# The output norm of a gated delta rule, per token block and head on ScalarE

## The chip, the cores and the metric

The kernel runs on one core of one Trainium2 chip. The metric is the device time of one execution in microseconds; for a kernel that runs several times it is the median of its runs. The core has five engines that work side by side, each through its own list of instructions in order: PE (TensorE, matmuls), DVE (VectorE), ACT (ScalarE), POOL (GpSimd) and SP (SyncE, which here issues the DMA transfers). An instruction starts when the one before it on its engine has started or ended and the semaphores that it waits for are set.

## The reference, cut to what matters

A decoder block of 512 tokens and 2048 channels: a projection of the normalised input, two parallel branches (sliding-window attention and a gated delta rule), a gated sum, an output projection and a last norm. The change is in the delta rule, which has 16 key heads, 32 value heads and chunks of 64 tokens. After the scan over the chunks every value head's output is normalised over its 128 channels:

```python
def rms_norm(x, w):
    xf = x.astype(jnp.float32)
    y = xf * lax.rsqrt(jnp.mean(xf * xf, axis=-1, keepdims=True) + EPS)
    return (y * w.astype(jnp.float32)).astype(x.dtype)

# scan over the chunks, state0 = 0
v_new = u_i - w_i @ state
o = (q_i * exp(g_i)) @ state + qk_i @ v_new
state = state * exp(g_last) + k_dec.T @ v_new

o_d = rms_norm(o_d, dn_norm_w[l]) * jax.nn.silu(z_d)
```

Since the first state is zero, the state after the first chunk is the product alone.

## The kernel before

All matmuls are done in float32 split in two parts: a weight tile of 128 x 1024 is loaded, cast on ACT to `whi` (L162), and the rest `wlo` is subtracted on POOL (L165; `lo_eng` is POOL in this stage). `mm_half` then runs 24 matmuls of 128 x 512 for it: eight with `whi` and the high part of the input (L174), eight with `whi` and its low part (L176), alternating, then eight with `wlo` (L179). Each of `w`, `whi` and `wlo` has three buffers.

PE's order is written out by the program. Side work runs as generators in `flow`: each matmul of a projection counts as one tick, and a generator that yields n goes on n ticks later. So the scan's small matmuls stand at fixed places between those of the projections. The other engines' lists are ordered by a scheduler that looks for what is ready, under `tc.high_priority()` sooner.

The stage of the change loops over 16 key heads `kh`, each with two value heads. While the projections for head kh+1 run, `scan(kh, ...)` goes through the eight chunks of head kh, both value heads side by side. A chunk c lies in token block T = c // 2 and does:

- L555 (PE): `pa` from the state `s_cur`; not in the first chunk.
- L562 (DVE): `rr`, and L566 (ACT): `xq`, both from `pa`. In the first chunk L570 (ACT) copies `rr`.
- L574 (PE): `pb`; L578 and L582 (DVE): `sv`; L585 (DVE), or L587 (ACT) in the first chunk: the output `o`.
- L591, L592 (PE): `pc`; L598 (DVE), or L601 (DVE) in the first chunk: the new state, tile `sn`.

After the last chunk `finish` does the norm over `o`, a tile of 128 tokens by 4 token blocks, 2 heads and 128 channels: square (L609, ACT, into `osq`), sum (L612, DVE, into `so`), a factor with the scale of q (L614, DVE), a reciprocal square root `ro` in ten small DVE steps of 128 x 8 (L193, and three times L195 to L197, in `rsqrt`), and the product of `o` and `ro` in place (L616, DVE). 36 ticks later PE transposes `o` (L621) and L627 multiplies it by the weight and the gate `zs`. The scan of the next head starts while this runs, so that its first chunks share DVE and ACT with `finish`. ACT also runs L295 and L643 (the value path), L649 (`zs`), L522, L524, L530 and L531 (`prepare`) and L288 (a gate tile after heads 3, 7 and 11); POOL copies `kc` (L511).

Of the kernel before, what the change touches and what calls it, by code (L numbers as in the profile page):

```python
# [8 lines left out]
F32 = mybir.dt.float32  # L9
F32R = mybir.dt.float32r  # L10
I32 = mybir.dt.int32
AF = mybir.ActivationFunctionType
ALU = mybir.AluOpType
AX = mybir.AxisListType

P = 128
S = 512
NT = S // P
# [61 lines left out]
def hybrid_block(  # L80
# [21 lines left out]
    pe, dve, act, pool = nc.tensor, nc.vector, nc.scalar, nc.gpsimd  # L102
# [10 lines left out]
    def new_pool(stack, name, bufs, side="left"):  # L113
        return stack.enter_context(tc.tile_pool(name=name, bufs=bufs, side=side, reuse_waits="tile"))
# [4 lines left out]
    def bank(tag, bufs=1):  # L119
        return ps.tile([P, S], F32, name=tag, bufs=bufs)  # L120
# [70 lines left out]
    def rsqrt(pl, y, v, n):  # L191
        t = pl.tile([P, n], F32, name="nrt")
        dve.tensor_scalar(y.bitcast(I32), v.bitcast(I32), -0.5, 1597463007.0, ALU.mult, ALU.add)  # L193
        for _ in range(3):
            dve.scalar_tensor_tensor(t, y, -0.5, v, ALU.mult, ALU.mult)  # L195
            dve.tensor_tensor(t, t, y, ALU.mult)
            dve.scalar_tensor_tensor(y, t, 1.5, y, ALU.add, ALU.mult)  # L197
# [288 lines left out]
    with ExitStack() as st:  # L486
        pv = new_pool(st, "pv", 2)
# [57 lines left out]
        def scan(kh, vb, zs):  # L545
            slab, tq, kth, ktl = got.pop(kh)
            o = pv.tile([P, NT, 2, P], F32, name="o")
            s_cur = None
            v2 = slice(2 * kh, 2 * kh + 2)
            for c in range(8):  # L550
                T, p = divmod(c, 2)
                rk, rq = (H0, H1) if p == 0 else (H1, H0)
                if c:
                    xp = bank("pa").rearrange("p (h e) -> p h e", h=4)[:, 0:2, :]
                    pe.matmul(xp, slab[:, T, 2 * p:2 * p + 2, :].rearrange("d b i -> d (b i)"), s_cur,  # L555
                              start=True, stop=True)
                    rr = rrs[p]
                    xq = pv.tile([P, 2, P], F32, name="xq")
                    with tc.high_priority():
                        for h in range(2):  # L560
                            vh = 2 * kh + h
                            dve.scalar_tensor_tensor(rr[rk, h, :], xp[rk, h, :], nbeG[rk, T, vh:vh + 1],  # L562
                                                     vb[rk, T, h, :], ALU.mult, ALU.add)
                    for h in range(2):
                        vh = 2 * kh + h
                        act.activation(xq[rq, h, :], xp[rq, h, :], AF.Copy, scale=eGs[rq, T, vh:vh + 1])  # L566
                    yield 8
                else:
                    rr = rrs[p]
                    act.copy(rr[rk], vb[rk, T])  # L570
                    yield 4
                yp = bank("pb").rearrange("p (h e) -> p h e", h=4)[:, 0:2, :]
                for h in range(2):
                    pe.matmul(yp[:, h, :], tq[:, h * 4 + T, :], rr[:, h, :], start=True, stop=True)  # L574
                if c < 7:
                    sv = pv.tile([P, 2, P], F32R, name="sv")
                    with tc.high_priority():
                        dve.tensor_tensor(sv[rk], yp[rk], eSuf[rk, T, v2].unsqueeze(2).broadcast_to([64, 2, P]),  # L578
                                          ALU.mult)
                        for h in range(2):  # L580
                            vh = 2 * kh + h
                            dve.scalar_tensor_tensor(sv[rq, h, :], yp[rk, h, :], eSuf[rk, T, vh:vh + 1],  # L582
                                                     sv[rk, h, :].bitcast(F32), ALU.mult, ALU.subtract)
                if c:
                    dve.tensor_tensor(o[rq, T], xq[rq], yp[rq], ALU.add)  # L585
                else:
                    act.copy(o[rq, T], yp[rq])  # L587
                yield 10
                if c < 7:
                    su = bank("pc").rearrange("p (h e) -> p h e", h=4)[:, 0:2, :]  # L590
                    pe.matmul(su, kth[:, T, p, :], sv, start=True, stop=False)  # L591
                    pe.matmul(su, ktl[:, T, p, :], sv, start=False, stop=True)  # L592
                    s_new = pv.tile([P, 2, P], F32, name="sn")
                    with tc.high_priority():
                        if c:
                            for h in range(2):
                                vh = 2 * kh + h
                                dve.scalar_tensor_tensor(s_new[:, h, :], s_cur[:, h, :], eTot[p][:, T, vh:vh + 1],  # L598
                                                         su[:, h, :], ALU.mult, ALU.add)
                        else:  # L600
                            dve.tensor_copy(s_new, su)  # L601
                    s_cur = s_new
                    yield 8
            flow.start(finish(kh, o, zs))

        def finish(kh, o, zs):
            osq = pv.tile([P, NT * 2, P], F32, name="osq", bufs=1)
            ov = o.rearrange("p t h e -> p (t h) e")
            act.activation(osq, ov, AF.Square)  # L609
            so = pv.tile([P, 8], F32, name="so")  # L610
            ro = pv.tile([P, 8], F32, name="ro")
            dve.tensor_reduce(so, osq, AX.X, ALU.add)  # L612
            so4 = so.rearrange("p (t h) -> p t h", h=2)
            dve.scalar_tensor_tensor(so4, so4, 1.0 / P, cq[:, :, kh:kh + 1].broadcast_to([P, NT, 2]), ALU.mult, ALU.add)  # L614
            rsqrt(pv, ro, so, 8)
            dve.tensor_tensor(ov, ov, ro.unsqueeze(2).broadcast_to([P, 8, P]), ALU.mult)  # L616
            yield 36
            for h in range(2):
                tp = bank("tr", 2)
                for T in range(NT):  # L620
                    pe.transpose(tp[:, T * P:(T + 1) * P], o[:, T, h, :], ident)  # L621
                od = pv.tile([P, S], F32, name="od")
                tv = tp.rearrange("p (t c i) -> p t c i", t=NT, c=2)
                dv = od.rearrange("p (t c i) -> p t c i", t=NT, c=2)
                zv = zs[:, h, :].rearrange("p (t c i) -> p t c i", t=NT, c=2)
                for p in range(2):
                    dve.scalar_tensor_tensor(dv[:, :, p, :], tv[:, :, 1 - p, :], dnw, zv[:, :, p, :], ALU.mult, ALU.mult)  # L627
                nc.sync.dma_start(od_d[KT + 2 * kh + h], od)
                yield 6
# [4 lines left out]
        for kh in range(NK):  # L634
            vb = pv.tile([P, NT, 2, P], F32, name="vb")
            zs = pv.tile([P, 2, S], F32, name="zs", bufs=3)
            flow.start(prepare(kh), 24 if kh else 60)
            for h in range(2):
                vh = 2 * kh + h

                def then(acc):
                    y = conv(acc, 32 + vh, pv)
                    act.activation(y, y, AF.Silu)  # L643
                    after = (lambda kh=kh, vb=vb, zs=zs: scans.add(scan(kh, vb, zs))) if h else None
                    flow.start(to_tokens(y, vb, h, vh, after))

                proj(w_in[T_DN + 32 + vh], then)
            for h in range(2):
                proj(w_in[T_DZ + 2 * kh + h], lambda acc: act.activation(zs[:, h, :], acc, AF.Silu))  # L649
                if h == 0 and kh + 1 < NK:  # L650
                    load_head(kh + 1)
            if kh in GATE_KH:
                gate_tile(pv, 47 - n_gate)
                n_gate += 1
# [339 lines left out]
```

## Time and profile before

| | us |
|---|---|
| median of 3 runs | 2913.93 (2913.84 to 2914.82) |
| profiled execution, its own time | 2914.18 |
| its span, first to last instruction | 2912.4 |
| PE busy | 2850.0 (98%) |
| DVE busy | 1762.9 (61%) |
| ACT busy | 1028.6 (35%) |
| POOL busy | 555.8 (19%) |
| delta-rule scan stage | 850 to 1830 of the span |

Matmuls overlap on PE: the busy time of one is longer than the distance to the next, and an idle PE is one that had no matmul in work. A row in order of time has the start in us, the duration in us, the engine, the line, the operation, output and input with their shapes, and xN where N rows were merged; in brackets stands how long the engine was idle before it and what ended that. A row of a group has, after the count, the total of its busy time in us and the mean of one in ns, then the idle time before it.

### The profile page before, as it was taken

The page shows a single profiled execution, that of the slowest core. Times are in us where ns is not written, and L with a number is a line of the kernel's source. Part 1 is how long each engine was busy: PE and PEld are TensorE (multiplying, and loading weights), DVE is VectorE, ACT ScalarE, POOL GpSimd, SP SyncE. Part 2 cuts the span into 40 slices and gives each one's busy share as a digit, 9 for nine tenths or more (in the row PEclk, how much of TensorE's full clock was granted, in tenths as well). Part 3 has the DMA queues.
Part 4 walks back from the last instruction along what each step waited for, and adds up shares of the span by engine and source line. Part 5 has one row for each costly group of instructions (what it writes and reads, how often), then busy time and mean ns, then how long its engine had stood idle before and what let it go on. Part 6 is the DMA issues. An engine that isn't in the chain of part 4 may idle for free.

```text
span 2912.4 us, 36773 instructions
## 1 busy us (share of the span) xinstructions
PE 2850.0 (98%) x13594; PEld 2370.9 (81%) x13594; DVE 1762.9 (61%) x3520; ACT 1028.6 (35%) x1645; POOL 555.8 (19%) x464
## 2 busy tenths in 40 slices
PE   7999999999999999999999999999999999999998
PEld 7778888888888888888878888877788888888887
DVE  6686667979825555555555554478884455455434
ACT  5532222232333343334333333355553222122222
POOL 2310000000033334333334333024230000000010
PEclk9999999999999999999999999999999999999999
DMA  3344444353553333333333322424237555554533
GB/s 132 115 123 142 135 136 151 125 207 116 174 153 100 103 110 103 105 98 116 98 109 109 104 89 94 133 87 113 91 109 225 172 174 163 156 163 147 181 100 103
DMA packets 184628, 376.07 MB, mean 129 GB/s; under 512 B 65505, under 2 KB 82273, under 8 KB 183041
## 3 DMA queue, kind: packets, MB, share of 16 engines
q1 hardware_dynamic: 184448, 373.72, 40.7%
q8 instruction: 108, 1.77, 0.3%
q14 instruction: 72, 0.58, 0.1%
HBM read 316.97 MB, written 54.59 MB: 128 GB/s over the span
## 4 chain that ended last, share of the span: by engine, by line
PE 88%; DVE 8%; ACT 2%; issue 1%; POOL 0%; DMA 0%; SPq 0%; ACTq 0%; DVEq 0%
PE acc L179 24%; PE acc L176 24%; PE acc L174 24%; PE pa L555 2%; PE pb L574 2%; PE fo L902 1%; PE fo L900 1%; PE fo L901 1%; PE acc L247 1%; PE tr L529 1%; DVE ptl L764 1%; DVE o L616 1%; DVE ro L197 1%; DVE wlo L165 1%; DVE ad L381 1%
## 5 line engine op out<-in xcount | busy, mean ns | idle before, releaser
L174 PE MATMUL acc<-hT_hi,whi 128*128 128x512 f32 x2592 | 1038.5, 401 | 0.0
L176 PE MATMUL acc<-hT_lo,whi 128*128 128x512 f32 x2592 | 1018.7, 393 | 0.0
L162 ACT CAST whi<-w 128x1024 fp32r<-128x1024 f32 x446 | 467.7, 1049 | 1166.5 <-PE acc L176 940.4
L179 PE MATMUL acc<-hT_hi,wlo 128*128 128x512 f32 x2592 | 685.1, 398 | 2.2 <-DVE wlo L165 2.2
L165 POOL TENSOR_TENSOR wlo<-w,whi 128x512 fp32r<-128x512 f32 x284 | 363.3, 1300 | 1231.8 <-PE acc L179 643.7
L165 DVE TENSOR_TENSOR wlo<-w,whi 128x512 fp32r<-128x512 f32 x608 | 424.0, 720 | 261.1 <-ACT whi L162 204.5
L176 PEld LDWEIGHTS acc<-hT_lo,whi 128*128 128x128 f32 x2592 | 488.6, 188 | 92.8
L174 PEld LDWEIGHTS acc<-hT_hi,whi 128*128 128x128 f32 x2592 | 488.3, 188 | 92.9
L179 PEld LDWEIGHTS acc<-hT_hi,wlo 128*128 128x128 f32 x2592 | 479.6, 188 | 98.1 <-DVE wlo L165 3.1
L176 PE MATMUL acc<-dl,whi 128*128 128x512 f32 x768 | 298.8, 389 | 0.0
L174 PE MATMUL acc<-dh,whi 128*128 128x512 f32 x768 | 298.8, 389 | 0.0
L179 PE MATMUL acc<-dh,wlo 128*128 128x512 f32 x768 | 189.7, 389 | 0.0
L297 DVE SCALAR_TENSOR_TENSOR cy<-acc,cw,cy 128x511 f32<-128x511 f32 (+2 forms) x192 | 142.8, 744 | 62.9 <-ACT cy L295 60.0
L863 DVE TENSOR_TENSOR gd<-acc,gl 128x512 f32<-128x512 f32 x80 | 55.3, 691 | 188.7 <-PE acc L179 188.7
L176 PEld LDWEIGHTS acc<-dl,whi 128*128 128x128 f32 x768 | 144.2, 188 | 30.0
L179 PEld LDWEIGHTS acc<-dh,wlo 128*128 128x128 f32 x768 | 144.1, 188 | 29.9
L174 PEld LDWEIGHTS acc<-dh,whi 128*128 128x128 f32 x768 | 144.1, 188 | 29.9
L562 DVE SCALAR_TENSOR_TENSOR rr<-pa,nbeG,vb 64x128 f32<-64x128 f32 x224 | 69.0, 348 | 143.2 <-PE pa L555 143.0
L920 POOL TENSOR_TENSOR y<-y,fw 128x512 f32<-128x512 f32 x12 | 18.9, 1605 | 658.7 <-ACT sqy L918 658.7
L566 ACT ACTIVATE xq<-pa,eGs 64x128 f32<-64x128 f32 x224 | 68.9, 356 | 170.1 <-DVE rr L562 167.6
L578 DVE TENSOR_TENSOR sv<-pb,eSuf 64x256 fp32r<-64x256 f32 x112 | 46.9, 418 | 116.7 <-PE pb L574 116.4
L467 DVE TENSOR_TENSOR m<-m,tm 128x62 f32<-128x62 f32 (+30 forms) x124 | 106.4, 858 | 2.8
(264 smaller groups left out, 3182.2 us busy)
## 6 DMA issues: line engine op xcount, KB each, us to landing
w<-w_in SPq DMA_DIRECT2D x326, 512.0 KB, 3.5
w<-w_dn SPq DMA_DIRECT2D x64, 512.0 KB, 3.5
gl<-ga_d SPq DMA_DIRECT2D x96, 256.0 KB, 2.6
w<-w_att SPq DMA_DIRECT2D x32, 512.0 KB, 3.8
w<-w_out SPq DMA_DIRECT2D x32, 512.0 KB, 3.5
of<-od_d SPq DMA_DIRECT2D x48, 256.0 KB, 3.9
kq_d<-slab SPq DMA_DIRECT2D x16, 512.0 KB, 2.8
ga_d<-gt SPq DMA_DIRECT2D x32, 256.0 KB, 3.8
```

The costliest lines, as they stand in the source:

```text
L162: act.copy(hi, w)
L165: lo_eng[0].tensor_sub(lo[:, r], w[:, r], hi[:, r].bitcast(F32))
L174: pe.matmul(acc, hi[:, k, :], rhi[k], start=first and k == 0, stop=False)
L176: pe.matmul(acc, hi[:, k, :], rlo[k], start=False, stop=False)
L179: pe.matmul(acc, lo[:, k, :], rhi[k], start=False, stop=last and k == n - 1)
L297: dve.scalar_tensor_tensor(y[:, sh:], acc[:, 0:S - sh], cw[:, t, 3 - sh:4 - sh], y[:, sh:], ALU.mult, ALU.add)
L467: dve.tensor_tensor(m[:, 0:jj, jj + 1:], m[:, 0:jj, jj + 1:], tm, ALU.add)
L555: pe.matmul(xp, slab[:, T, 2 * p:2 * p + 2, :].rearrange("d b i -> d (b i)"), s_cur, start=True, stop=True)
L562: dve.scalar_tensor_tensor(rr[rk, h, :], xp[rk, h, :], nbeG[rk, T, vh:vh + 1], vb[rk, T, h, :], ALU.mult, ALU.add)
L566: act.activation(xq[rq, h, :], xp[rq, h, :], AF.Copy, scale=eGs[rq, T, vh:vh + 1])
L574: pe.matmul(yp[:, h, :], tq[:, h * 4 + T, :], rr[:, h, :], start=True, stop=True)
L863: dve.tensor_tensor(gd, acc, gl, ALU.mult)
```

## The change

Three edits, all in the scan stage:

- The square of `finish` becomes eight instructions on ACT, one for each token block and head (128 x 128), each of which also gives the sum over its channels as a column of `so`; the sum on DVE goes.
- The product of `o` and `ro` becomes eight instructions on ACT, each with its column of `ro` as scale; the product on DVE goes.
- The copy of the first state of each head goes from DVE to ACT.

```diff
                         else:
-                            dve.tensor_copy(s_new, su)
+                            act.copy(s_new, su)
 ...
         def finish(kh, o, zs):
-            osq = pv.tile([P, NT * 2, P], F32, name="osq", bufs=1)
             ov = o.rearrange("p t h e -> p (t h) e")
-            act.activation(osq, ov, AF.Square)
             so = pv.tile([P, 8], F32, name="so")
             ro = pv.tile([P, 8], F32, name="ro")
-            dve.tensor_reduce(so, osq, AX.X, ALU.add)
+            for n in range(8):
+                osq = pv.tile([P, P], F32, name="osq", bufs=2)
+                act.activation(osq, ov[:, n], AF.Square, accum_out=so[:, n:n + 1])
             so4 = so.rearrange("p (t h) -> p t h", h=2)
             dve.scalar_tensor_tensor(so4, so4, 1.0 / P, cq[:, :, kh:kh + 1].broadcast_to([P, NT, 2]), ALU.mult, ALU.add)
             rsqrt(pv, ro, so, 8)
-            dve.tensor_tensor(ov, ov, ro.unsqueeze(2).broadcast_to([P, 8, P]), ALU.mult)
+            for n in range(8):
+                act.activation(ov[:, n], ov[:, n], AF.Copy, scale=ro[:, n:n + 1])
```

The new squares stand at L612 and the new products at L617 of the changed kernel; lines behind `finish` have a number higher by one (L644 for L643, L650 for L649, L628 for L627). PE's order is the same row for row. Those of ACT and DVE change where `finish` of one head meets the start of the next.

ACT, where `finish` of head 0 meets the first chunk of head 1, before:

```order
L566 ACTIVATE xq<-pa,eGs 64x128 x2
L609 ACTIVATE osq<-o 128x1024
L570 COPY rr_6246<-vb 64x256
L162 CAST whi<-w_7137 128x1024
L587 COPY o<-pb 64x256
L649 ACTIVATE zs<-acc 128x512
L566 ACTIVATE xq<-pa,eGs 64x128 x2
```

and now, where `w_7157` is the same weight tile as `w_7137`:

```order
L566 ACTIVATE xq<-pa,eGs 64x128 x2
L612 ACTIVATE osq,so<-o 128x128 x2
L570 COPY rr_6246<-vb 64x256
L617 ACTIVATE o<-o,ro 128x128 x8
L587 COPY o<-pb 64x256
L650 ACTIVATE zs<-acc 128x512
L162 CAST whi<-w_7157 128x1024
L601 COPY sn<-pc 128x256
L566 ACTIVATE xq<-pa,eGs 64x128 x2
```

The last two of the eight squares stay there (the other six went forward into the scan), the eight products come in ahead of L587 and `zs`, the weight cast goes behind them, and the state's copy is last. At the next head's `finish` (head 1) the cast stands ahead of the products, and after head 2 `zs` does so too.

DVE at the same place (head 0 to head 1), before:

```order
L612 TENSOR_REDUCE so<-osq 128x8
L614 SCALAR_TENSOR_TENSOR so<-so,cq 128x8
L193 TENSOR_SCALAR ro<-so 128x8
...
L578 TENSOR_TENSOR sv<-pb,eSuf 64x256
L195 SCALAR_TENSOR_TENSOR nrt<-ro,so 128x8
L582 SCALAR_TENSOR_TENSOR sv<-pb,eSuf,sv 64x128 x2
L196 TENSOR_TENSOR nrt<-nrt,ro 128x8
L197 SCALAR_TENSOR_TENSOR ro<-nrt,ro 128x8
L616 TENSOR_TENSOR o<-o,ro 128x1024
L601 COPY sn<-pc 128x256
L562 SCALAR_TENSOR_TENSOR rr_6247<-pa,nbeG,vb 64x128 x2
```

and now:

```order
L614 SCALAR_TENSOR_TENSOR so<-so,cq 128x8
L193 TENSOR_SCALAR ro<-so 128x8
...
L195 SCALAR_TENSOR_TENSOR nrt<-ro,so 128x8
L196 TENSOR_TENSOR nrt<-nrt,ro 128x8
L197 SCALAR_TENSOR_TENSOR ro<-nrt,ro 128x8
L578 TENSOR_TENSOR sv<-pb,eSuf 64x256
L582 SCALAR_TENSOR_TENSOR sv<-pb,eSuf,sv 64x128 x2
L562 SCALAR_TENSOR_TENSOR rr_6247<-pa,nbeG,vb 64x128 x2
```

Reduce, product and state copy are gone, and `sv` (L578, L582), which stood among the last small steps of `rsqrt`, now stands behind all of them.

## Prediction

> **What bounds the kernel now.** I read the page first, then the busy times by stretch, then TensorE's waits in one stretch, and last the rows in order of time around one such wait. All sums are against the profiled execution: 2914.18 us, 1.8 us around its span, and 0.25 us above the median 2913.93 us. Its span:
>
> ```profile
> span 2912.4 us, 36773 instructions
> ```
>
> The edit lies in the scan of the delta rule, which runs from about 850 to 1830 us. Columns: length of the stretch, then busy us of PE, PEld, DVE, ACT, POOL, and the granted clock:
>
> ```profile
> 850.00:1830.00 980.00, 962.15 (x4817) 801.49 (x4816) 539.65 (x1338) 364.91 (x608) 357.29 (x290) 1.00 0.34 103
> ```
>
> TensorE is idle for 17.85 of 980 us at full clock, so no edit of vector work can win much more than that here. Who makes it wait (us in total, times, longest):
>
> ```profile
> PE pa L555 <- DVE sn L601: 13.2, 12, 1.5
> PE pc L591 <- DVE sv L582: 4.2, 5, 1.2
> ```
>
> So nearly all of it is one wait: the second chunk of a head wants the first state, sn, that L601 copies. I call the point where `finish` of head kh runs while head kh+1 starts a changeover, and sort the 16 by kh modulo 4: A (0, 4, 8, 12), B (1, 5, 9, 13), C (2, 6, 10, 14), D (3, 7, 11), and the last head. The 12 waits sit in A, B and C; D, after a gate tile, has none. The first A, engine by engine:
>
> ```profile
> 912.63 0.41 DVE L585 TENSOR_TENSOR o<-xq,pb 64x256 f32<-64x256 f32 x1 [1.74 <-PE pb L574]
> ...
> 914.17 1.22 DVE L612 TENSOR_REDUCE so<-osq 128x8 f32<-128x1024 f32 x1 [0.48 <-ACT osq L609]
> 915.43 0.17 DVE L614 SCALAR_TENSOR_TENSOR so<-so,cq 128x8 f32<-128x8 f32 x1
> 915.63 0.17 DVE L193 TENSOR_SCALAR ro<-so 128x8 int32<-128x8 int32 x1
> ...
> 918.27 1.17 DVE L197 SCALAR_TENSOR_TENSOR ro<-nrt,ro 128x8 f32<-128x8 f32 x1
> 919.48 2.27 DVE L616 TENSOR_TENSOR o<-o,ro 128x1024 f32<-128x1024 f32 x1
> 921.67 0.41 DVE L601 COPY sn<-pc 128x256 f32<-128x256 f32 x1
> ```
> ```profile
> 913.08 1.06 ACT L609 ACTIVATE osq<-o 128x1024 f32<-128x1024 f32 x1 [1.48 <-DVE o L585]
> ...
> 915.80 1.05 ACT L162 CAST whi<-w 128x1024 fp32r<-128x1024 f32 x1 [1.36 <-issue]
> 918.13 0.37 ACT L587 COPY o<-pb 64x256 f32<-64x256 f32 x1 [1.28 <-DVE sv L582]
> 918.52 0.60 ACT L649 ACTIVATE zs<-acc 128x512 f32<-128x512 f32 x1
> ```
> ```profile
> 913.76 0.60 POOL L511 COPY kc<-slabv 128x512 f32<-128x512 f32 x1
> ...
> 918.13 2.54 POOL L165 TENSOR_TENSOR wlo<-w,whi 128x512 fp32r<-128x512 f32 x2 [3.76 <-issue]
> ```
> ```profile
> 920.58 0.39 PE L176 MATMUL acc<-hT_lo,whi 128*128 128x512 f32 x1
> 922.13 0.70 PE L555 MATMUL pa<-sn,slabv 128*128 128x256 f32 x2 [1.17 <-DVE sn L601]
> 922.48 0.59 PE L174 MATMUL acc<-hT_hi,whi 128*128 128x512 f32 x1
> ```
>
> VectorE runs in order. Reduce, eleven small steps (one each 0.20 us) and the scaling L616 stand ahead of L601, which ends at 922.08, while ScalarE has nothing to do after 919.12. TensorE's own loss is more than the 1.17 us shown. The same step where it does not wait:
>
> ```profile
> 863.69 0.39 PE L176 MATMUL acc<-hT_lo,whi 128*128 128x512 f32 x1
> 863.91 0.59 PE L555 MATMUL pa<-sn,slabv 128*128 128x256 f32 x2
> 864.16 0.59 PE L174 MATMUL acc<-hT_hi,whi 128*128 128x512 f32 x1
> ```
>
> There L555 starts 0.22 us after L176 and L174 0.25 us after that; in A it is 1.55 and 0.35. The loss is 1.33 + 0.10 = 1.43 us: each wait costs about 0.27 us more than its row says. L555 was wanted at 920.58 + 0.22 = 920.80.
>
> Two of VectorE's rows are stretched: L197 took 1.17 and L616 2.27 while POOL's wlo ran (918.13 to 920.67).
>
> ```profile
> L197 DVE SCALAR_TENSOR_TENSOR ro<-nrt,ro x48: 166/166/1220, 916.2 to 1823.8; 128x8 f32<-128x8 f32 x48
> L616 DVE TENSOR_TENSOR o<-o,ro 128x1024 f32<-128x1024 f32 x16 | 23.8, 1486 | 0.5
> ```
>
> A step of 166 ns that takes up to 1220 ns looks held until the POOL operation beside it (1.27 us each) ends. The Trainium skill ("SBUF — State Buffer", Who interferes with whom) says that a VectorE instruction with two SBUF inputs and a GpSimd one that reads SBUF fully block each other, and that ScalarE never waits on anyone. The rows above agree. By that rule the scaling on ScalarE is never held; were it held there as L616 was, by 1.05 us, the four A would give 4.2 us less.
>
> **The change, priced.** Removed from VectorE per head: L612 1.22, L616 1.49 and L601 0.41 us, 50 us in all, of which only what stands before L601 in A, B and C is on TensorE's path. Added on ScalarE; the nearest rows:
>
> ```profile
> L918 ACT ACTIVATE sqy<-y 128x512 f32<-128x512 f32 x15 | 9.4, 628 | 25.2 <-DVE y L916 25.2
> L733 ACT ACTIVATION_READ_ACCUMULATOR sc<-sc,nm 128x1 f32 x128 | 23.9, 187 | 0.0
> L934 ACT ACTIVATE y<-y,rsf 128x512 f32<-128x512 f32 x8 | 5.3, 716 | 9.2 <-DVE rsf L209 9.2
> ```
> ```profile
> 2873.02 1.34 ACT L934 ACTIVATE y<-y,rsf 128x512 f32<-128x512 f32 x2 [2.33 <-DVE rsf L209]
> ```
>
> - Square: 1.06 us at 1024 elements (L609) and 0.628 at 512 give 0.85 ns per element, so 0.30 us at 128, and 0.187 for the read of the sum. Two L934 take 1.34 rather than 1.43, so neighbours overlap by 0.09: 0.31 us per square with its read. Six of a head's eight run while its scan goes on; only two wait for its last block.
> - Scale: 0.716 - 384 x 0.00085 = 0.39 us, 0.30 from one to the next; eight take 2.4 us. Ends: 0.26 (were the overlap larger) and 0.39 (none); I take 0.30, the nearest row's own.
> - State copy: as L587, the same 256 elements per partition out of PSUM, 0.37 us.
>
> ScalarE's busy time rises by 16 x (8 x 0.49 + 8 x 0.39 - 1.06 + 0.37), about 102 us, to 467 of 980. That is covered: the casts L162 run when one of three buffers comes free, two weight tiles ahead of TensorE (24 matmuls, 0.22 us apart as in the rows above, are 5.3 us per tile), so A's cast, which moves from 915.80 to 919.8, is not seen. Without that cover each late cast would cost its lateness. The transposes that read o stand 36 ticks after `finish`; o is ready at 919.0 in A, not at 921.75. POOL's and SP's orders stay, and the order holds 31 table loads before and after.
>
> Now the sn time in each class, in the new order. **A**: o is done at 913.04, two squares and reads until 913.8; if POOL's L511 (until 914.36) holds the first small step, eleven steps end at 916.6. Scales to 919.0; L587, zs and the weight cast, which now stands between zs and sn, start at 919.0, 919.3 and 919.8; sn 920.75 to 921.1, against 920.80 wanted: 0.3 late, a loss of 0.4 instead of 1.43.
>
> **B and C** (first of each):
>
> ```profile
> 972.34 0.41 DVE L585 TENSOR_TENSOR o<-xq,pb 64x256 f32<-64x256 f32 x1 [0.76 <-PE pb L574]
> ...
> 1032.13 0.41 DVE L585 TENSOR_TENSOR o<-xq,pb 64x256 f32<-64x256 f32 x1 [1.46 <-PE pb L574]
> ```
> ```profile
> 974.14 1.05 ACT L162 CAST whi<-w 128x1024 fp32r<-128x1024 f32 x1 [0.29 <-PE acc L176]
> ...
> 1034.81 0.60 ACT L649 ACTIVATE zs<-acc 128x512 f32<-128x512 f32 x1 [0.24 <-PE acc L179]
> ...
> 1105.45 0.60 ACT L649 ACTIVATE zs<-acc 128x512 f32<-128x512 f32 x1 [0.81 <-PE acc L179]
> ```
> ```profile
> 976.47 2.54 POOL L165 TENSOR_TENSOR wlo<-w,whi 128x512 fp32r<-128x512 f32 x2 [3.01 <-issue]
> ```
> ```profile
> 979.83 0.39 PE L176 MATMUL acc<-hT_lo,whi 128*128 128x512 f32 x1
> 981.29 0.70 PE L555 MATMUL pa<-sn,slabv 128*128 128x256 f32 x2 [1.07 <-DVE sn L601]
> ...
> 1041.56 0.70 PE L555 MATMUL pa<-sn,slabv 128*128 128x256 f32 x2 [1.53 <-DVE sn L601]
> ...
> 1107.31 0.59 PE L555 MATMUL pa<-sn,slabv 128*128 128x256 f32 x2
> ...
> 1768.76 0.38 PE L591 MATMUL pc<-sv,kth 128*128 128x256 f32 x1 [1.21 <-DVE sv L582]
> ```
>
> B: squares end 973.5, ro 975.75, before POOL's wlo at 976.47; scales to 978.2, L587, zs, sn done 979.4; wanted 980.05. C: ro 1035.5, after zs; scales to 1037.95, sn done 1038.6; wanted about 1039.9. D: sn follows zs, done 1106.35; wanted 1107.31. So B and C lose their waits and D gets none. Head 14, a C, waits at L591 (1.21) and 0.27 at L555, because small steps were held; the new order puts sv behind all eleven steps and the same POOL operation falls among them, so I give it half back.
>
> **Sum**: A 4 x (1.43 - 0.40) = 4.1; B 4 x (1.07 + 0.27) = 5.4; C three waits that with head 14's 0.27 make 13.2 - 4 x 1.17 - 4 x 1.07, so 4.0, plus 3 x 0.27 = 4.8; head 14 half of 1.21 + 0.27 + 2 x 0.27 = 1.0. Together 15.3 us: 2914.18 - 15.3 = 2898.9, or 2898.6 as a median. The other four L591 waits stay: they come from head preparation.
>
> **Rivals.** A difference under 0.2% (5.8 us) can hardly be told from none here.
>
> 1. *All of it goes*: A isn't late, head 14 is clean (17.9 us saved) and the four other L591 waits vanish with VectorE's lighter load (4 x 1.0). 2892. For it: A misses by only 0.3. Against: those four follow a cast held by POOL. 12%.
> 2. *Between*: scales don't overlap (0.39, 0.7 us later): A loses 1.1, B 0.2, about 11 saved, 2903; up to 2908 if part of the copy also waits for a cast. 12%.
> 3. *The wait changes engines*: sn now stands behind eight scales in order, as it stood behind L616. If ScalarE's chain is 1.5 us later than I have it, A loses 1.9 (4 x 0.5 more than now), B 0.95, C 0.3, and D, short of 0.55, gets a wait of 0.65 thrice: net 2 us, 2912, no change. The Trainium skill ("ScalarE: Activation LUTs", Rules for kernel authors) says to multiply on VectorE and not on ScalarE, which speaks for this rival; by rows, 2.4 us for eight scales against 1.22 for an unheld L616 agrees that ScalarE is slower, and only its idle time saves the change. 12%.
> 4. *Slower, by POOL's hold*: the eleven small steps stay on VectorE and sv now stands behind all of them. From 0.7 us later than I have them, B's and C's last steps meet both wlo operations (976.47 to 979.01 in B): sv ends about 980.1, L591 waits 2.1 us, then L555 0.3. B loses 2.8 instead of 1.34, C about 2.9 instead of 1.6; with A's 4.1 saved that is 5.6 lost, 2919.5. Head 14's row shows that it happens. 8%.
>
> **Chances.** The likeliest, at 56%, is 2898.6, with 2895 to 2903 as its own range. Cases 1 and 2 make it 80% for 2891.5 to 2908, the range; 3 and 4 are left out. Faster by over 0.2%: 56 + 12 + 12 = 80%; within: 14% (case 3 and part of 4); slower 6%.
>
> **What would show it.** L555 has no wait on sn in B and C, and 0 to 0.4 us in A; squares of about 0.30 and scales of about 0.39 us; the eleven steps end before wlo starts in B; TensorE idle 3 to 6 us in the stretch, not 17.85. It would be wrong if L591 waits for sv in B or C, if L555 waits in D, if scales start more than 1 us after ro, or if TensorE starts to wait for a weight cast.

## The result, and the profile after

| | before | changed |
|---|---|---|
| median, us | 2913.89 (2912.09 to 2914.82, 4 runs) | 2899.11 (2897.90 to 2899.86, 4 runs) |
| ratio, 95% interval | | 0.995, 0.9935 to 0.9966 |
| profiled execution, its own time | 2914.18 | 2897.90 |

The change makes the kernel 14.8 us faster (2913.89 - 2899.11), and the interval of the ratio lies below 1. The forecast was 2898.6 us. Of the five runs behind the median of 2896.86 us in the table of the experiments, one took 3154.43 us at a granted clock of 0.849; the other four lie between 2895.78 and 2897.40 us. The page of the changed kernel begins:

```profile
span 2896.1 us, 37062 instructions
```

The scan stage, with the columns as before (length, then busy us of PE, PEld, DVE, ACT, POOL, then the granted clock):

```profile
850.00:1830.00 980.00, 975.26 (x4884) 814.16 (x4883) 484.02 (x1297) 438.77 (x995) 351.74 (x289) 1.00 0.35 106
```

VectorE has 56 us less to do than before, ScalarE 74 more, and TensorE is idle for 4.74 us of the 980 instead of 17.85. TensorE's waits in the stage (us in total, times, longest):

```profile
PE pc L591 <- DVE sv L582: 3.5, 5, 0.7
PE pa L555 <- ACT sn L601: 0.8, 4, 0.2
```

Twelve waits of 13.2 us for sn have become four of 0.8 us. The groups of the new instructions on ScalarE (total of busy time, mean of one in ns, idle time before):

```profile
L617 ACT ACTIVATE o<-o,ro 128x128 f32<-128x128 f32 x128 | 39.2, 389 | 16.1 <-DVE ro L197 15.7
L612 ACT ACTIVATE osq<-o 128x128 f32<-128x128 f32 x128 | 38.8, 304 | 97.5 <-DVE o L585 97.2
L612 ACT ACTIVATION_READ_ACCUMULATOR osq<-o 128x1 f32 x128 | 23.9, 187 | 0.0
L601 ACT COPY sn<-pc 128x256 f32<-128x256 f32 x16 | 5.9, 370 | 0.1
```

The first A in order of time, on VectorE, ScalarE and TensorE:

```profile
910.06 0.41 DVE L585 TENSOR_TENSOR o<-xq,pb 64x256 f32<-64x256 f32 x1 [1.74 <-PE pb L574]
...
911.23 0.58 DVE L614 SCALAR_TENSOR_TENSOR so<-so,cq 128x8 f32<-128x8 f32 x1
...
913.66 0.17 DVE L197 SCALAR_TENSOR_TENSOR ro<-nrt,ro 128x8 f32<-128x8 f32 x1
914.08 0.42 DVE L578 TENSOR_TENSOR sv<-pb,eSuf 64x256 fp32r<-64x256 f32 x1 [0.25 <-PE pb L574]
```
```profile
913.87 2.46 ACT L617 ACTIVATE o<-o,ro 128x128 f32<-128x128 f32 x8 [2.31 <-DVE ro L197]
916.35 0.37 ACT L587 COPY o<-pb 64x256 f32<-64x256 f32 x1
916.74 0.60 ACT L650 ACTIVATE zs<-acc 128x512 f32<-128x512 f32 x1
917.23 1.04 ACT L162 CAST whi<-w 128x1024 fp32r<-128x1024 f32 x1
918.17 0.38 ACT L601 COPY sn<-pc 128x256 f32<-128x256 f32 x1
```
```profile
918.01 0.39 PE L176 MATMUL acc<-hT_lo,whi 128*128 128x512 f32 x1
918.59 0.70 PE L555 MATMUL pa<-sn,slabv 128*128 128x256 f32 x2 [0.20 <-ACT sn L601]
```

VectorE now has nothing but eleven small steps ahead of sv, and sv waits for its own input. ScalarE is the engine on which sn stands last: eight scales, a copy (L587), the gate `zs` and a weight cast, 4.3 us without a gap. sn ends at 918.54 and L555 waits 0.20 us for it.

### The profile page after: what moved, and what is told of

Its sections match the earlier page's. It is cut to its first block, busy times and chain, and to the rows that moved or that the text cites. A ratio compares the mean times of both kernels' runs of the same rounds, so it can differ in the third digit from the quotient of the medians.

```text
span 2896.1 us, 37062 instructions
## 1 busy us (share of the span) xinstructions
PE 2845.1 (98%) x13594; PEld 2368.0 (82%) x13594; DVE 1703.8 (59%) x3472; ACT 1098.7 (38%) x2029; POOL 552.4 (19%) x464
## 4 chain that ended last, share of the span: by engine, by line
PE 91%; DVE 5%; ACT 2%; issue 1%; POOL 0%; DMA 0%; ACTq 0%; DVEq 0%
PE acc L179 25%; PE acc L176 25%; PE acc L174 25%; PE pb L574 2%; PE pa L555 2%; PE fo L902 1%; PE fo L901 1%; PE fo L903 1%; PE acc L247 1%; PE tr L529 1%; DVE ptl L765 1%; PE pc L591 1%; DVE ad L381 1%; DVE wlo L165 1%; PE tr L622 0%
## 5 line engine op out<-in xcount | busy, mean ns | idle before, releaser
L578 DVE TENSOR_TENSOR sv<-pb,eSuf 64x256 fp32r<-64x256 f32 x112 | 47.0, 419 | 119.4 <-PE pb L574 119.2
```

## The experiments

The prediction took VectorE's order as given and asked what stands ahead of sn. It left open which part of the change is needed, and why VectorE was late at all. Theory: sn is late by what stands ahead of it on its engine, so each part alone is enough and the parts do not add up. Rivals: VectorE's load is what counts; or the copy itself has to leave VectorE. The medians and ratios come from runs beside the kernel before; the last three columns are read from each profile. The waits are those that the profile lists, and it lists no idle time below 0.15 us. Listed waits for other tiles come to 1.3 us in the kernel with the scales twice and to 0.6 us at most in the others.

| kernel | median, us | ratio to before, 95% interval | L555, first to last, us | waits of L555, us (times) | waits of L591 |
|---|---|---|---|---|---|
| before | 2913.4 to 2914.5 | | 951.3 | 13.2 (12) | 4.2 (5) |
| the change | 2899.11 | 0.9935 to 0.9966 | 936.7 | 0.8 (4) | 3.5 (5) |
| copy alone | 2898.59 | 0.9937 to 0.9962 | 936.2 | 0 | 4.2 (6) |
| squares and scales, no copy | 2896.86 | 0.9927 to 0.9954 | 934.6 | 0 | 3.5 (5) |
| scales alone | 2899.37 | 0.9937 to 0.9962 | 936.3 | 0 | 4.1 (5) |
| squares alone | 2899.05 | 0.9933 to 0.9960 | 936.5 | 0 | 4.8 (5) |
| the change, scales twice | 2923.86 | 1.0022 to 1.0046 | 961.7 | 19.3 (12) | 3.8 (6) |
| squares, scales and ktl's copies | 2892.54 | 0.9912 to 0.9939 | 930.3 | 0 | 0.7 (1) |
| the change, wlo on VectorE | 2891.27 | 0.9908 to 0.9935 | 929.9 | 0 | 0 |
| before, wlo on VectorE | 2888.75 | 0.9899 to 0.9926 | 927.4 | 0 | 0 |
| copy alone, wlo on VectorE | 2889.53 | 0.9901 to 0.9928 | 927.7 | 0 | 0 |
| squares, scales, ktl, wlo on VectorE | 2890.05 | 0.9904 to 0.9931 | 928.2 | 0 | 0 |

The column of L555 is the distance between the first and the last of its 224 matmuls in the stage, as in these two rows (before, then changed); what happens ahead of the stage is not in it:

```profile
L555 PE MATMUL pa<-sn,slabv x224: 376/377/483, 863.9 to 1815.2; 128*128 128x256 f32 x112
```
```profile
L555 PE MATMUL pa<-sn,slabv x224: 377/377/484, 861.4 to 1798.1; 128*128 128x256 f32 x112
```

**One part at a time.** The copy alone, on the kernel before:

```diff
-                            dve.tensor_copy(s_new, su)
+                            act.copy(s_new, su)
```

> The kernel before with one edit: the first state copy sn of a head (L601) is made on ScalarE; squares, norm and scales stay on VectorE. Theory (only what stands ahead of sn on its own engine counts): sn now stands right behind the two small ScalarE operations of the head and comes before it is wanted in every class of changeover, so all twelve waits of L555 go: 13.2 us and twelve restarts of 0.27 us, 16.4 us in all, about 2897.5 us, a little below the change itself; L591's waits for sv stay as before, head 14's among them. Rival (VectorE's load in the changeover is what counts, and one copy is 0.2 us of it): less than 3 us saved, about 2911 us.

It saved 15.9 us (2914.47 - 2898.59). No wait of L555 is left, and all that TensorE waits for sv stays (total, times, longest):

```profile
PE pc L591 <- DVE sv L582: 4.2, 6, 1.2
```

sn now ends 1.25 to 1.27 us before L555 starts in every A, B and C. So one copy of 0.37 us, moved to an engine where it does not stand behind the norm, gives as much as the whole change. The other way round, the changed kernel with that copy back on VectorE:

```diff
-                            act.copy(s_new, su)
+                            dve.tensor_copy(s_new, su)
```

> The changed kernel with one part undone: squares with their sums and the scales are on ScalarE, but the first state copy sn stays on VectorE. Theory: with the eight scales and the square gone from VectorE, sn stands behind the eleven small steps and sv alone, at about 919.6 us in the first changeover, 1.2 us before it is wanted; the waits of L555 go, head 14's wait halves: about 2897 us. Rival (the copy has to leave VectorE): about 2913 us.

17.6 us saved; the copy does not have to leave. Then the scales alone on ScalarE (squares, sum and copy as before):

```diff
-            dve.tensor_tensor(ov, ov, ro.unsqueeze(2).broadcast_to([P, 8, P]), ALU.mult)
+            for n in range(8):
+                act.activation(ov[:, n], ov[:, n], AF.Copy, scale=ro[:, n:n + 1])
```

> The kernel before with one edit: the eight scales of a finished block are on ScalarE; square, sum and the first state copy stay on VectorE. Theory: sn comes right behind ro, about 2.5 us earlier than before: in time in class A (saves 4 x 1.43 = 5.7 us), 0.05 us late in B (saves about 4.6 us), 0.4 us late in C (saves about 3.3 us); some 13.6 us in all, about 2900.3 us. Rival (the parts of the change add up, and this one is a third of it): about 2909 us.

15.1 us saved, 1.5 more than forecast: B and C were to be late by 0.05 and 0.4 us. B is in time, with 0.09 us between the end of sn and L555. In the first C L555 starts 0.06 us after sn ends, which is the distance that it has in the waits of before too (0.05 to 0.06 us), so there sn is still late, by about 0.1 us, too little to be listed. The first B on VectorE:

```profile
973.99 1.22 DVE L197 SCALAR_TENSOR_TENSOR ro<-nrt,ro 128x8 f32<-128x8 f32 x1
...
975.65 0.17 DVE L197 SCALAR_TENSOR_TENSOR ro<-nrt,ro 128x8 f32<-128x8 f32 x1
975.73 0.42 DVE L601 COPY sn<-pc 128x256 f32<-128x256 f32 x1
```

The small step is still held at 1.22 us, and sn is just in time all the same. Last, the squares with their sums alone on ScalarE, the scales and the copy on VectorE:

> The kernel before with one edit: the eight squares with their sums are on ScalarE; the scales and the first state copy stay on VectorE, the scales now ahead of sv in VectorE's order. Theory: VectorE is done with the scales early and sn still comes in time, so L555's waits go; but sv stands behind the scales, so if anything holds the scales (1.22 us on paper), L591 waits for sv instead: about 2897.5 us if not held, up to 1.5 us for each of eleven changeovers more if held, 2897 to 2914 us. Rival (the parts add up): about 2909 us, with both waits shortened but none gone.

15.4 us saved. L555 waits nowhere. The scaling stands ahead of sv in every A, B and C and takes 1.22 us there. The price named for sv fell on head 14 only, where two small steps ahead of the scaling are held (L591 waits 2.0 us, the longest of its waits in any kernel here):

```profile
1748.77 1.29 DVE L195 SCALAR_TENSOR_TENSOR nrt<-ro,so 128x8 f32<-128x8 f32 x1
1750.10 1.22 DVE L196 TENSOR_TENSOR nrt<-nrt,ro 128x8 f32<-128x8 f32 x1
...
1751.55 1.22 DVE L616 TENSOR_TENSOR o<-o,ro 128x1024 f32<-128x1024 f32 x1
1752.69 0.41 DVE L578 TENSOR_TENSOR sv<-pb,eSuf 64x256 fp32r<-64x256 f32 x1
```

The parts alone give 15.9, 15.1 and 15.4 us, together 14.8. They do not add up; each brings sn to TensorE in time or nearly so, and coming earlier than that wins nothing.

**How near the change is to its limit.** The scales made twice, and the first copy taken out of its priority so that the scheduler keeps it behind all sixteen:

```diff
+            for n in range(8):
+                osq = pv.tile([P, P], F32, name="osq", bufs=2)
+                act.activation(osq, ov[:, n], AF.Copy, scale=ro[:, n:n + 1])
             for n in range(8):
                 act.activation(ov[:, n], ov[:, n], AF.Copy, scale=ro[:, n:n + 1])
```

> The changed kernel with each scale made twice on ScalarE (first into a scratch tile, then in place), and the first state copy without its priority, so that it stays behind all sixteen scales. ScalarE gets 2.45 us more per head, 39 us in all, and stays under half busy. Theory (what stands ahead of sn on its engine, by the margins of the changed kernel's trace): class A had a wait of 0.20 and loses 2.45 less the 0.95 of one weight cast that now stands behind sn, 1.5 each, 6.0 in four; B had a margin of 0.59 and waits 1.86 more and a restart of 0.27, 8.5 in four; C had 1.10 and waits 1.35 and a restart, 4.9 in three; head 14 had none and loses 2.45; class D's rr copy stands behind the scales and may cost 0 to 1.3 each. Together 22 to 26 us: 2921 to 2925 us, slower than the kernel before. Rival (ScalarE is idle more than half the time and has room): 2899 us.

2923.86 us, 10.5 above the kernel before (2913.36 beside it), within the forecast. ScalarE is busy for 464.50 of 980 us:

```profile
850.00:1830.00 980.00, 955.17 (x4769) 794.43 (x4769) 476.18 (x1284) 464.50 (x1100) 351.89 (x289) 1.00 0.32 102
```
```profile
PE pa L555 <- ACT sn L601: 19.3, 12, 2.4
```

The single waits were 1.64 to 1.66 us in A (1.7 forecast), 1.70 in B (1.86), 1.18 to 1.20 in C (1.35) and 2.36 in head 14 (2.45). An engine that is idle more than half the time costs 25 us against the change when one copy stands behind 2.45 us more of other work in each head.

**Why VectorE was late.** The four L591 waits of head preparation were put down to a cast held beside GpSimd. On the kernel with squares and scales moved, ktl's casts go to ScalarE:

```diff
-                dve.tensor_copy(ktl[r2, :, p, :], ktl[r, :, p, :].bitcast(F32))
                 yield 8
+            for p, r, r2 in ((0, H0, H1), (1, H1, H0)):
+                act.copy(ktl[r2, :, p, :], ktl[r, :, p, :].bitcast(F32))
```

> The kernel with squares and scales on ScalarE and the state copy on VectorE (the best so far), and the two copies of ktl to the other half of the partitions (L525) made on ScalarE too, behind the second copy of kth. Theory: the four remaining waits of L591 in the head preparation come from L525, which VectorE takes 1.15 us for beside GpSimd's wlo and 0.42 us otherwise, with sv behind it; with L525 gone they go, 4 x (0.69 + 0.27) = 3.8 us, and on ScalarE it is not held (about 0.6 us each): about 2893 us. Rival (the second subtraction of ktl, which stands between sv's two instructions, is what makes sv late): under 1.5 us saved, 2895.5 us or more.

2892.54 us; the four waits are gone and head 14's is left (the edit moves the lines by one, so L592 here is L591). But the edit did more than the forecast says. In the changed kernel, the first of the four places on VectorE:

```profile
994.90 1.14 DVE L525 CAST ktl<-ktl 64x512 fp32r<-64x512 f32 x1
996.07 0.43 DVE L578 TENSOR_TENSOR sv<-pb,eSuf 64x256 fp32r<-64x256 f32 x1
996.42 0.69 DVE L523 TENSOR_TENSOR ktl<-tr,kth 64x512 fp32r<-64x512 f32 x1
997.14 0.63 DVE L582 SCALAR_TENSOR_TENSOR sv<-pb,eSuf,sv 64x128 fp32r<-64x128 f32 x2
```

The second subtraction of ktl (L523, 0.69 us) stands between the two instructions of sv, as the rival says, and with the cast gone the scheduler puts it behind both, at all four places. The hold (1.14 - 0.42 = 0.72 us) and L523 are each as long as the wait (0.69 us), so this kernel does not tell the theory from the rival, though its time is the one that the theory gave.

What TensorE still waits for sv, and the casts on ScalarE, where each takes the same time, whatever runs beside it (ns: least, median, most):

```profile
PE pc L592 <- DVE sv L583: 0.7, 1, 0.7
```
```profile
L527 ACT CAST ktl<-ktl x32: 612/616/619, 843.1 to 1711.9; 64x512 fp32r<-64x512 f32 x32
```

Then the other side of the same pair: in the changed kernel, GpSimd's wlo goes to VectorE, which has 284 more instructions for it.

```diff
-        lo_eng[0] = pool
+        lo_eng[0] = dve
```

> The changed kernel with the low parts of the weights (L165) on VectorE instead of GpSimd in this stage: 284 instructions of 0.685 us, some 195 us more on VectorE. Theory (a VectorE instruction with two SBUF inputs is held while GpSimd's wlo runs): no small step of the norm and no L525 is longer than 0.2 and 0.43 us any more (up to 1.29 and 1.17 us now). The time is the price of the load on VectorE and is not forecast closer than 2895 to 2960 us. Rival (the long ones are long for another reason): they stay at 1.2 us.

The first run gave 2891.94 us, and the median of five with it is 2891.27:

> The changed kernel with L165 on VectorE in this stage, timed in rounds beside the others: 2892 us as in its one run, since the five waits of L591 are gone and two waits of L555 of 0.2 us are left.

The cast on VectorE, in the kernel before and in this one:

```profile
L525 DVE CAST ktl<-ktl x30: 420/424/1164, 883.8 to 1732.7; 64x512 fp32r<-64x512 f32 x30
```
```profile
L525 DVE CAST ktl<-ktl x30: 420/422/425, 883.1 to 1713.0; 64x512 fp32r<-64x512 f32 x30
```

No instruction of the norm is longer than 0.62 us any more. The forecast of 0.2 us for all of them was too strict: GpSimd still makes `kc` (L511, 0.61 us), and some steps meet it. This shows the hold itself: with wlo off GpSimd, the long casts and steps are gone. It does not single out the cast as the cause of the four waits of L591, since here too L523 no longer stands between the instructions of sv.

The profile of the first run lists two waits of 0.2 us for sn, that of the timed kernel none for sn or sv. But in its four A sn is still late, by too little to be listed (the first of them):

```profile
918.86 0.37 ACT L601 COPY sn<-pc 128x256 f32<-128x256 f32 x1
```
```profile
919.28 0.70 PE L555 MATMUL pa<-sn,slabv 128*128 128x256 f32 x2
```

L555 starts 0.05 us after sn ends, as in the waits. ScalarE's chain ahead of sn is the one of the changed kernel, and the hold has no part in it. The distance of the L555 fell by 6.8 us (936.7 - 929.9). PE's order is the same row for row in all these kernels, so the distances from one start to the next can be compared: L591 and L592 start 5.6 us closer to what stands ahead of them, L555 0.9 us, of which the four A have 0.4.

So the question became whether the change was needed. The same one line on the kernel before, norm and copy all on VectorE:

> The kernel before, with the low parts of the weights (L165) on VectorE instead of GpSimd in this stage; norm, scales and state copy stay on VectorE as before. VectorE's load rises from 540 to some 720 us of the 990. Theory (sn was late because GpSimd's wlo held the small steps and the scale ahead of it): by the rows of before the holds ahead of sn are 2.05 us in the first changeover, 1.48 in the second and 1.97 in the third, and one wlo of 0.72 us now stands among them, so sn comes 1.3, 0.8 and 1.25 us earlier: waits of L555 gone in A, 0.3 left in B, up to 0.3 left in C; with the four L591 waits of the head preparation gone too, about 2896 to 2900 us, as good as the change itself. Rival (VectorE has too much work in the changeover, whoever holds it): more load, so slower than before, 2920 us or more.

2888.75 us, 25.4 below before, better than the change and better than forecast. The rival's load is there; VectorE is busy for 680.92 us of the 980 instead of 539.65, and TensorE without a gap:

```profile
850.00:1830.00 980.00, 980.00 (x4924) 822.67 (x4924) 680.92 (x1623) 371.70 (x615) 9.97 (x18) 1.00 0.33 109
```

The first A on VectorE, to be held against the rows of before (L197 1.17, L616 2.27):

```profile
917.89 0.17 DVE L197 SCALAR_TENSOR_TENSOR ro<-nrt,ro 128x8 f32<-128x8 f32 x1
918.00 0.69 DVE L165 TENSOR_TENSOR wlo<-w,whi 128x512 fp32r<-128x512 f32 x1
918.61 1.22 DVE L616 TENSOR_TENSOR o<-o,ro 128x1024 f32<-128x1024 f32 x1
919.75 0.42 DVE L601 COPY sn<-pc 128x256 f32<-128x256 f32 x1
```
```profile
920.42 0.59 PE L555 MATMUL pa<-sn,slabv 128*128 128x256 f32 x2
```

From the reduce to sn the order is that of before, with one wlo more in it, in all four A, and sn is there 0.25 us early instead of 1.28 us late. In A, then, the hold by GpSimd was the whole of the lateness. In B and C it cannot be told as cleanly: with wlo on VectorE the scheduler also puts sn ahead of the last small steps and L616, so there the margins of about 1.1 and 0.7 to 0.9 us come from the order too. By the rows of before, the holds ahead of sn (1.48 us in the first B, 1.97 in the first C) are longer than its lateness (1.18 and 1.65 us); that they alone make it late there is an estimate from these rows and not shown.

The last two kernels combine the line with the copy, and with squares, scales and ktl:

> The kernel before with two edits: the first state copy on ScalarE, and L165 on VectorE in this stage. Theory: the waits of L555 go by the first (15.9 us measured alone), the waits of L591 by the second (four of 0.69 and a restart of 0.27, and head 14's 1.21), about 2892 us. Rival (VectorE, with reduce, scales and wlo all on it, becomes late for something else): 2897 us or more.

> Squares, scales and ktl's copies on ScalarE, the state copy on VectorE, L165 on VectorE in this stage. Theory: no wait of L555 or L591 is left in the stage, 2891 to 2892 us, less than 1 us below each of the two it is made of, since their gains are the same waits. Rival (the gains of the ktl copies and of L165 add up): 2887 us.

2889.53 and 2890.05 us, both below their forecasts, and no wait is listed in either. Once GpSimd is out of the way, moving the norm adds nothing: gains are the same waits and do not add up.

The one line on the kernel before saved 23.9 us in the L555 column, more than the 17 listed waits with their restarts (17.4 + 17 x 0.27 = 22.0). Compared start by start as above, L555 gives 16.6 us of it, L591 and L592 7.5, and all other matmuls lose 0.2. The surplus lies with L591 and L592: beside the five listed waits, sixteen L591 of before start 0.06 to 0.16 us later than here, too little to be listed. The other kernels with wlo on VectorE differ from this one in the same way: the change with it is 2.6 us longer, 1.4 at L555, in the four A, and 1.3 at L591 and L592; squares, scales and ktl 0.8 us longer, 1.0 at L591 and L592; the copy 0.2 us longer. So an empty list of waits does not mean that nothing is late.

## Why the prediction was right, by its own steps

The rows of L555 after heads 0, 1, 2 and 3, and the one ahead of them:

```profile
861.36 0.59 PE L555 MATMUL pa<-sn,slabv 128*128 128x256 f32 x2
...
976.47 0.59 PE L555 MATMUL pa<-sn,slabv 128*128 128x256 f32 x2
...
1034.97 0.59 PE L555 MATMUL pa<-sn,slabv 128*128 128x256 f32 x2
...
1100.62 0.59 PE L555 MATMUL pa<-sn,slabv 128*128 128x256 f32 x2
```

With 918.59 above, these rows are 2.55, 3.54, 4.82, 6.59 and 6.69 us earlier than the same rows of before (863.91, 922.13, 981.29, 1041.56, 1107.31). The steps between them are what each class gained.

- **A**: 0.99 measured, 1.03 forecast. sn was forecast to end 0.3 us after it is wanted and does so by 0.31 (918.54 against 918.01 + 0.22); the listed 0.20 us is only the time in which TensorE had no matmul in work. The chain held row by row: eleven steps ended at 913.83 (forecast 916.6 on the clock of before, on which the changed kernel is 2.55 us ahead here: 914.05), with L614 held at 0.58 us by `kc`.
- **B**: 1.28 measured, 1.34 forecast. Margin 0.59 us, 0.65 forecast.
- **C**: 1.77 measured in the first, 1.80 forecast from its row (1.53 + 0.27). Margin 1.10 us, 1.3 forecast.
- **D**: 0.10 measured, none forecast. No wait.
- **Head 14**: the half that was a guess. L591 waits 0.73 us instead of 1.21, and a wait of L555 is no longer listed; counted start by start it gained about 0.8 us, not 1.0. The reason given was right: two small steps meet wlo.

```profile
1748.15 1.29 DVE L195 SCALAR_TENSOR_TENSOR nrt<-ro,so 128x8 f32<-128x8 f32 x1
1749.48 1.22 DVE L196 TENSOR_TENSOR nrt<-nrt,ro 128x8 f32<-128x8 f32 x1
```
```profile
1748.13 2.53 POOL L165 TENSOR_TENSOR wlo<-w,whi 128x512 fp32r<-128x512 f32 x2 [4.32 <-ACT whi L162]
```

- **The sum**: the distance of the L555 fell by 14.6 us (951.3 - 936.7), 15.3 forecast; the medians by 14.8. The span fell by 16.3, and 2.55 of that is no part of the change, since it lies ahead of the stage. In the first 60 us the profiled execution of before had a granted clock of 0.97, that of the changed kernel 1.00 (columns as in the stage's row).

```profile
0.00:60.00 60.00, 43.45 (x305) 41.99 (x306) 34.31 (x77) 32.62 (x42) 18.59 (x16) 0.97 0.45 159
```
```profile
0.00:60.00 60.00, 42.32 (x325) 40.70 (x326) 36.21 (x80) 33.88 (x44) 18.59 (x16) 1.00 0.43 159
```

The clock cannot be the whole reason: the kernel with the scales twice had 0.94 there and its first L555 at 861.45, as early as the changed kernel. The rest stays open.

- **Prices**: square 304 ns (0.30), read 187 (187), scale 389 (0.39), eight scales 2.46 us (2.4), copy 370 (0.37). Wrong was ScalarE's busy time: 438.77 us, not 467. The step added up the lengths of neighbours that overlap; with the pitches that the same text gives (0.31 and 0.30) it would have been 16 x (8 x 0.31 + 2.4 - 1.06 + 0.37), 67 us more and not 102. 74 came. Nothing hung on it.
- **The bound**: "TensorE is idle for 17.85 of 980 us, so no edit of vector work can win much more than that here" was too low. The idle time leaves out the restarts and the small delays, and the one line that moved wlo won 23.9 us in this stage.
- **The signs**: scales start 0.04 us after `ro` in the first A and as closely in the first B and C; the eleven steps of the first B end at 972.12, ahead of wlo at 972.88; L555 does not wait in D; among the changeovers L591 waits for sv at head 14 alone.
- **Rival 1** (all goes, 2892) did not come by the change, but is the time of the kernels without the hold. Its objection held: the four waits stayed, and each follows a held cast, though L523 between the instructions of sv may have as large a part in them. **Rival 3** is shown as a mechanism by the doubled scales: the wait does change engines once ScalarE's chain is longer than the margin, and the change has 0.59 us of it in B and none in A. The rule of the Trainium skill behind it ("ScalarE: Activation LUTs", Rules for kernel authors: multiply on VectorE) decides nothing here, since scales alone (2899.37 us), copy alone (2898.59) and the whole change (2899.11) give the same time. **Rival 4** has its place: sv behind a held chain, in head 14 only.

What the prediction did not ask is what the hold cost before. It quoted the rows (L197 1.17, L616 2.27, together 2.05 us longer than unheld, with sn 1.28 us late) and used them only to bound the change. sn was late because it stood behind the norm and because the norm was held. In A it is shown that taking either away is enough; in B and C the kernel without the hold has another order as well.

## What to carry to other kernels

Before work is moved off a late engine, look in its rows for instructions that take several times their usual length, and at what ran beside them: here one line that took the other party away gave 25 us, and moving the norm 15, though the order that the scheduler made of the rest changed with it. When several edits shorten the same queue, their gains do not add up; the first that brings the awaited result under its deadline takes nearly all, and the margin left is the number to know. A busy share says little: an engine idle for half the stage cost 25 us by what stood ahead of one copy in its order.

## What the runs showed of the hardware

In these rows GpSimd and VectorE held each other, and who came first went on. In the kernel before, L616 started 0.04 us ahead of GpSimd in a D, kept its 1.22 us, and two wlo took 3.58 us instead of 2.53:

```profile
1098.67 1.22 DVE L616 TENSOR_TENSOR o<-o,ro 128x1024 f32<-128x1024 f32 x1
```
```profile
1098.71 3.58 POOL L165 TENSOR_TENSOR wlo<-w,whi 128x512 fp32r<-128x512 f32 x2 [2.42 <-ACT whi L162]
```

The hold was not limited to instructions with two tensors from SBUF: L193 (one input, 128 x 8) and the cast L525 were held to 1.22 and 1.16 us, while the reduce L612 kept its length in all sixteen heads:

```profile
L612 DVE TENSOR_REDUCE so<-osq x16: 1219/1220/1221, 914.2 to 1819.6; 128x8 f32<-128x1024 f32 x16
```

What read PSUM was not held. In the stage of the kernel before, 80 instructions of L582, 44 of L578 and 44 of L598 started while a wlo ran, and they kept their usual lengths (0.33 to 0.36, 0.40 to 0.43 and 0.34 to 0.35 us). Of the norm, which reads SBUF alone, 26 small steps and four L616 did, and every one was stretched (the small steps to 0.58 us or more). So sv and sn were not held themselves, but stood behind what was.

The Trainium skill ("SBUF — State Buffer", Who interferes with whom) has these points: casts and tensor_scalar may enter the mode that takes the shared ports, tensor_reduce never contends on trn2, and the order of issue decides who blocks. These rows agree; that no reduce met a wlo, only `kc` for up to 0.57 us, makes the last row the weaker evidence. The Trainium skill's page "Perfetto Trace Analysis" (Optimizing Scalar/DVE Operations) warns that moving work between GpSimd and VectorE might not help for that reason; here wlo takes 0.69 us on VectorE and 1.27 us on GpSimd, and moving it to VectorE was the best single line tried.
